# Output product of a state-space mixer: 128 rows of stacked real and imaginary parts, or 64 rows of each part

## Chip, cores and metric

One NeuronCore of a Trainium2 chip runs the whole program in one launch. The metric is the device time of that launch in microseconds (us). Engines: PE (TensorE, matmuls; PEld is its weight load), DVE (VectorE), ACT (ScalarE), POOL (GpSimd) and SP, whose queue issues all the DMAs named here.

## What is computed

One layer of a hybrid decoder on a prompt of 2048 tokens and 8 single-token samples, width 1024. The input projection feeds a state-space mixer (512 channels), a pooling mixer (512 channels) and a gate for each; an output projection, a residual and a LayerNorm follow. The change lies in the state-space mixer, which is complex and diagonal: 32 groups of 16 channels with 64 states each.

```python
bu_re = jnp.einsum('blgc,gnc->blgn', ug, bbar_re)
bu_im = jnp.einsum('blgc,gnc->blgn', ug, bbar_im)
_, _, hr, hi = lax.associative_scan(_scan_combine, (a_re, a_im, bu_re, bu_im), axis=1)
...
y = (jnp.einsum('blgn,gcn->blgc', hr, c_re.astype(f32))
     - jnp.einsum('blgn,gcn->blgc', hi, c_im.astype(f32)))
y = y.reshape(bsz, L, SSM_WIDTH) + d.astype(f32) * u
```

Here `hr`, `hi` are the states' real and imaginary parts, and both contribute to the output `y`.

## The kernel before

**Stages.** Rows of x are transposed on PE into `xh`/`xl` (each number is held as a high and a low part, and a product takes three matmuls: high by high, high by low, low by high, the list `HL`). The projection `proj` (L207) then runs tile by tile for the whole first two thirds of the program. Beside it run side tasks: `params` builds the mixer's weights, `ssm_task` the state-space mixer, `pool_diff` and `pool_gate` the pooling mixer. After 470 us come the GLU (L1058) and the output projection with LayerNorm (L1098).

**Order.** The schedule of PE, ACT, DVE and POOL is the order in which the code emits instructions. `Line` counts the matmul time emitted so far and lets each side task go on when its next due time (the numbers it yields) has come. Each engine then executes its own list strictly in that order; only SP's queue is ordered by the framework.

**The mixer.** The 2048 tokens are 256 blocks of 8 tokens. `ssm_task` goes through 16 pairs of groups (`gp`). For each pair: `ssm_load` fetches block inputs `ut` and weights by DMA; `ssm_uh` splits `ut` into high and low (`uh`, ACT L155 then DVE L149); `ssm_s` multiplies them by `ws` (PE, L629) into the block sums `s`; four ACT copies (L684) bring `s` into `SP` in the scan's layout: partition 64c+n is state n of group c of the pair, and dim 1 holds the real and imaginary part. POOL copies the sample columns to `bus` (L690). DVE rotates (`SP`, `B`), scans over the blocks in four pieces (L722, start values L716 and L718), and rotates back: two products over all 128 partitions, and then the four half-size sums that make the states `hf`:

```python
o = [hf[64 * a:64 * a + 64, c, 9:265] for c in range(2) for a in range(2)]
tt(o[0], A[p0, 0], B[p0, 1], ALU.subtract, G)
tt(o[1], A[p0, 1], B[p0, 0], ALU.add)
tt(o[2], A[p1, 0], B[p1, 1], ALU.subtract)
tt(o[3], A[p1, 1], B[p1, 0], ALU.add)
```

These move the layout: partition 64a+n of `hf` holds part a (real, imaginary) of state n, and dim 1 the group. The first runs on POOL (`G`), the other three on DVE. `hf` is split into `hh` (ACT, then DVE), and `ssm_out` (L642) multiplies `hh` by the output weights `wq` into the PSUM pair `py`, where L704 has already put the part that comes from the block's own inputs. For each group that is one product over 128 partitions, real and imaginary part stacked, so 6 matmuls of 264 columns per pair. The next pair's `uh` and `s` are emitted between scan and `hh`, and `ssm_out` of a pair comes in the scan of the next. `wq` comes from the DRAM tensor `qw_d` (4 DMAs per pair, L711), written in `params` (8 DMAs, L451). `hsh` holds the samples' start states in the layout of `hf` (L674, L735).

Of the kernel before, what the change touches and what calls it, by code (L numbers as in the profile page):

```python
# [9 lines left out]
F32 = mybir.dt.float32  # L10
# [3 lines left out]
ALU = mybir.AluOpType  # L14
# [3 lines left out]
P = 128  # L18
# [27 lines left out]
class Line:  # L46
    """Emission order: side tasks advance as the matmuls of the main stream go by."""
# [38 lines left out]
class Lock:  # L86
    """One holder at a time among the side tasks."""
# [14 lines left out]
def hybrid_step(  # L102
# [39 lines left out]
    qw_d = dram.tile([2, NST, 2, GP, 2, P], F32, name="qw_d")  # L142
# [15 lines left out]
    def cmul(out, a, z, m1, m2, sh, eng=None):  # L158
        """out = a * z, complex; a and out hold (re, im) in dim 1, z is a pair of broadcast views."""
        tt(m1, a, z[0].to_broadcast(sh), ALU.mult, eng)  # L160
        tt(m2, a, z[1].to_broadcast(sh), ALU.mult, eng)
        tt(out[:, 0], m1[:, 0], m2[:, 1], ALU.subtract, eng)
        tt(out[:, 1], m1[:, 1], m2[:, 0], ALU.add, eng)
# [57 lines left out]
    def params(tmp, prod):  # L221
# [183 lines left out]
        for g0 in range(0, GP, N2):  # L405
# [28 lines left out]
            for g in range(2):  # L434
# [16 lines left out]
            dma(out=qw_d[:, :, :, g2].rearrange("p n a g h c -> (p n) a (g h c)"),  # L451
                in_=QH.rearrange("p a g h c -> p a (g h c)").bitcast(F32))
# [186 lines left out]
    def ssm_out(gp, py, hh, wq):  # L639
        for c in range(2):  # L640
            for i, (a, b) in enumerate(HL):
                nc.tensor.matmul(out=py[:, c, 0:264], lhsT=wq[:, c, a], rhs=hh[:, b, c], start=False, stop=(i == 2))  # L642
        line.t += 0.66
        yt = sc_["sc"].tile([P, 2, 264], F32, tag="yt", name=f"yt{gp}")
        S.activation(out=yt, in_=py[:, :, 0:264], func=AF.Gelu_apprx_tanh)
        for c in range(2):
            g = 2 * gp + c
            dma(out=y_d[:, CH * g:CH * g + CH, :], in_=yt[:, c, 8:264])
        dma(out=ys_d[2 * gp:2 * gp + 2].rearrange("g c b -> c g b"), in_=yt[0:CH, :, 0:8])

    def ssm_task():
# [6 lines left out]
        bus, hs0, hsh = (sc.tile([P, 2, NB, GP], F32, name=nm) for nm in ("bus", "hs0", "hsh"))  # L658
        ssm_load(0)
        srt = sc.tile([P, 4, P], F32, tag="hh", name="srt")  # L660
        srh = srt[:, 2:4].rearrange("p a (i n) -> p a i n", i=2)
        for i, st in enumerate((state_re, state_im)):
            dma(out=srt[:, i], in_=st[0].rearrange("b (a c) n -> (b a) (c n)", c=2))
            dma(out=srh[:, :, i], in_=st[0].rearrange("b (a c) n -> (b a) c n", c=2))
# [6 lines left out]
        for i in range(4):  # L671
            transpose(ph[:, P * i:P * i + P], srt[:, i], P)
        S.copy(out=hs0.rearrange("p a b g -> p (a b g)"), in_=ph[:, 0:256])
        S.copy(out=hsh.rearrange("p a b g -> p (a b g)"), in_=ph[:, 256:512])  # L674
# [3 lines left out]
        p0, p1 = slice(0, 64), slice(64, 128)  # L678
        for gp in range(GP):
# [17 lines left out]
            for h in range(NCK // HC):  # L697
                if h == 0 and prev:
                    ssm_out(*prev)
                if h == 2:  # L700
# [8 lines left out]
                    for c in range(2):  # L709
                        for a in range(2):  # L710
                            dma(out=wq[64 * a:64 * a + 64, c].bitcast(F32), in_=qw_d[c, :, a, gp])  # L711
# [18 lines left out]
            o = [hf[64 * a:64 * a + 64, c, 9:265] for c in range(2) for a in range(2)]  # L730
            tt(o[0], A[p0, 0], B[p0, 1], ALU.subtract, G)
            tt(o[1], A[p0, 1], B[p0, 0], ALU.add)
            tt(o[2], A[p1, 0], B[p1, 1], ALU.subtract)
            tt(o[3], A[p1, 1], B[p1, 0], ALU.add)
            S.copy(out=hf[:, :, 0:8], in_=hsh[:, :, :, gp])  # L735
# [25 lines left out]
        for a, o, f in ((0, o_re_s, o_re_p), (1, o_im_s, o_im_p)):  # L761
            dma(out=o[0].rearrange("b (a c) n -> (b a) (c n)", c=2), in_=hout[:, a])
            dma(out=f[0, 0].rearrange("(a c) n -> a c n", c=2),
                in_=fout[:, :, NST * a:NST * a + NST])
# [133 lines left out]
    def pool_seq(gi, seq, hook):  # L898
        """seq: (0, i) reads chunk i of the pooled part, (1, i) of its gate."""
# [329 lines left out]
```

## Time and profile before

| what | us |
|---|---|
| median of 3 runs (lowest, highest) | 725.35 (725.2, 725.85) |
| span of the profiled execution | 721.6 |
| lies around the span, if it ran like one of the three | 3.6 to 4.25 |
| PE busy in the span | 679.6 (94%) |
| DVE busy | 513.0 (71%) |
| ACT busy | 230.9 (32%) |
| POOL busy | 210.0 (29%) |

The span reaches from the first to the last instruction; the time of that execution as a whole is not listed by itself. A busy share is an average over stages with different limits, so the stage of the mixer has to be read by itself. "L642" is a line of the kernel before.

### The profile page before, as it was taken

The numbers are of one execution on the slowest core, as the hardware profiler recorded it, in microseconds if no ns is written. First come the engines' busy times: TensorE is split into PE (matmuls) and PEld (weight loads), VectorE is DVE, ScalarE is ACT, GpSimd is POOL, SyncE is SP. The second block draws the span as 40 slices with busy tenths as digits, with TensorE's granted clock in tenths as the row PEclk, the third lists the DMA queues.
The fourth block names the chain that finished last, engine by engine and source line by source line (L and its number), as shares of the span: only waits on it lengthen the run. The fifth ranks groups of instructions, "written<-read, shape, count | busy, mean of one in ns | idle before, by whom it ended". The sixth has DMA issues, their size and how long they took to land.

```text
span 721.6 us, 10736 instructions
## 1 busy us (share of the span) xinstructions
PE 679.6 (94%) x3641; PEld 576.5 (80%) x3641; DVE 513.0 (71%) x1145; ACT 230.9 (32%) x472; POOL 210.0 (29%) x266
## 2 busy tenths in 40 slices
PE   6999999999999999979988989989999999999995
PEld 5987887888898879867876778776888868888884
DVE  3699888652789899988988895487555557646444
ACT  4442233233433333333333232354221323313100
POOL 2006435300010222222134223655313234051322
PEclk9999999999999999999998999999999999999998
DMA  8992778665555343433343224944455562634432
GB/s 286 215 355 79 173 205 206 175 226 163 165 158 163 107 141 115 139 101 102 119 131 107 86 75 122 366 146 104 111 118 137 128 174 60 148 90 115 118 87 60
DMA packets 134902, 105.99 MB, mean 147 GB/s; under 512 B 71459, under 2 KB 112551, under 8 KB 134839
## 3 DMA queue, kind: packets, MB, share of 16 engines
q1 hardware_dynamic: 134847, 105.30, 51.6%
q8 instruction: 29, 0.48, 0.3%
q14 instruction: 26, 0.21, 0.1%
HBM read 63.82 MB, written 41.68 MB: 146 GB/s over the span
## 4 chain that ended last, share of the span: by engine, by line
PE 45%; DVE 24%; ACT 5%; DMA 3%; issue 3%; POOL 2%; SPq 2%; DVEq 0%; ACTq 0%; POOLq 0%
PE o L1098 24%; PE pj L207 14%; PE z L1058 5%; DVE SP L149 4%; DVE hf L149 3%; DVE B L722 3%; POOL ws L149 2%; DVE B L149 2%; ACT SP L684 2%; DVE ini L718 2%; DVE uh L149 1%; DMA wst<-in_w_in_dram 1%; DVE w L149 1%; DVE dh L149 1%; PE os L1098 1%
## 5 line engine op out<-in xcount | busy, mean ns | idle before, releaser
L207 PE MATMUL pj<-xh,w 128*128 128x512 f32 (+2 forms) x1312 | 334.2, 348 | 0.0
L207 PEld LDWEIGHTS pj<-xh,w 128*128 128x128 f32 x1312 | 225.2, 190 | 28.7
L207 PE MATMUL pj<-xl,w 128*128 128x512 f32 (+2 forms) x656 | 206.4, 346 | 0.0
L1098 PE MATMUL o<-wo,mix 128*128 128x512 f32 (+1 forms) x792 | 176.9, 384 | 1.5 <-ACT mix L155 1.5
L1098 PEld LDWEIGHTS o<-wo,mix 128*128 128x128 f32 x792 | 145.1, 188 | 32.5 <-ACT mix L155 2.3
L207 PEld LDWEIGHTS pj<-xl,w 128*128 128x128 f32 x656 | 120.0, 189 | 14.1
L149 POOL TENSOR_TENSOR xr<-xr,gb 128x1024 f32<-128x1024 f32 x15 | 36.0, 2401 | 48.1 <-DVE xr L149 42.7
L149 POOL TENSOR_TENSOR hf<-SP,B 64x256 f32<-64x256 f32 x16 | 15.4, 960 | 108.6 <-DVE B L149 108.6
L1058 PE MATMUL z<-yh,w_g 128*128 128x512 f32 (+2 forms) x240 | 45.4, 348 | 0.0
L1087 ACT ACTIVATE xr<-xr,mv 128x1024 f32<-128x1024 f32 x15 | 18.7, 1245 | 79.4 <-DVE mv L1077 74.6
L1058 PEld LDWEIGHTS z<-yh,w_g 128*128 128x128 f32 x240 | 38.7, 188 | 6.3 <-issue 0.2
L1066 DVE SCALAR_TENSOR_TENSOR xr<-xr,o 128x512 f32<-128x512 f32 (+1 forms) x33 | 22.0, 667 | 26.1 <-PE o L1098 26.1
L149 POOL TENSOR_TENSOR ws<-ws 128x525 f32<-128x525 f32 (+5 forms) x30 | 37.8, 1259 | 3.3 <-DVE dh L149 1.1
L149 POOL TENSOR_TENSOR ws<-pc 128x527 f32<-128x527 f32 (+1 forms) x20 | 20.4, 1018 | 56.8 <-ACT pc L813 20.3
L155 ACT CAST hh<-hf 128x528 fp32r<-128x528 f32 x16 | 10.1, 634 | 76.5 <-DVE hf L149 72.6
L149 DVE TENSOR_TENSOR xl<-pt,xh 128x1024 fp32r<-128x1024 f32 (+1 forms) x17 | 19.8, 1164 | 16.5 <-ACT xh L155 16.2
L149 POOL TENSOR_TENSOR mv<-mv,mhalf 128x1 f32<-128x1 f32 x16 | 9.9, 619 | 74.2 <-DVE mv L1072 74.2
L722 DVE TENSOR_TENSOR_SCAN B<-r,ini,SP 128x64 f32<-128x64 f32 x96 | 29.9, 353 | 0.0
L149 DVE TENSOR_TENSOR hf<-SP,B 64x256 f32<-64x256 f32 x48 | 28.4, 591 | 1.0
L149 DVE TENSOR_TENSOR yh<-y,yh 128x512 fp32r<-128x512 f32 (+2 forms) x20 | 12.2, 610 | 21.6 <-ACT yh L155 19.1
L149 DVE TENSOR_TENSOR mix<-y,mix 128x512 fp32r<-128x512 f32 (+2 forms) x20 | 18.3, 915 | 12.1 <-ACT mix L155 12.1
L690 POOL COPY bus<-SP 128x16 f32<-128x16 f32 x16 | 8.8, 550 | 60.3 <-ACT SP L684 60.3
(220 smaller groups left out, 915.9 us busy)
## 6 DMA issues: line engine op xcount, KB each, us to landing
wst<-in_w_in_dram SPq DMA_DIRECT2D x16, 512.0 KB
xr<-in_x_prompt_dram SPq DMA_DIRECT2D x24, 256.0 KB
out_dram<-xr SPq DMA_DIRECT2D x22, 256.0 KB
xw<-in_x_prompt_dram SPq DMA_DIRECT2D x8, 512.0 KB
wt_d<-wzero SPq DMA_DIRECT2D x4, 1024.0 KB
sw_d<-sv SPq DMA_DIRECT2D x8, 512.0 KB
qw_d<-qh SPq DMA_DIRECT2D x8, 512.0 KB
ws<-sw_d SPq DMA_DIRECT2D x16, 256.0 KB
```

The costliest lines, as they stand in the source:

```text
L149: (eng or V).tensor_tensor(out=out, in0=a, in1=b, op=op)
L155: S.copy(out=hi, in_=src)
L207: nc.tensor.matmul(out=ps[:, :n], lhsT=w[:, a, k], rhs=xcols(b, k, t0, n), start=(i == 0), stop=(i == 23))
L684: S.copy(out=SP[64 * c:64 * c + 64, a], in_=ps[64 * a:64 * a + 64, c, 0:264])
L690: G.tensor_copy(out=bus[:, :, :, gp], in_=SP[:, :, 256:264])
L718: V.scalar_tensor_tensor(out=it[:, a], in0=e[:, 1 - a], scalar=z7[:, 2 - a, gp:gp + 1], in1=it[:, a], op0=ALU.mult, op1=ALU.add)
L722: V.tensor_tensor_scan(out=B4[:, a, h], data0=dec, data1=A4[:, a, h], initial=ini[a], op0=ALU.mult, op1=ALU.add)
L1058: nc.tensor.matmul(out=ps[:, :n], lhsT=w[:, a, k, P * (m % 2):P * (m % 2) + P], rhs=yh[:, b, k, :n], start=(i == 0), stop=(i == 11))
L1066: V.scalar_tensor_tensor(out=xt[:n, c], in0=xt[:n, c], scalar=ALPHA, in1=ps, op0=ALU.mult, op1=ALU.add)
L1087: S.activation(out=xt[:n], in_=xt[:n], func=AF.Identity, scale=mv[:n, 2:3], bias=mv[:n, 0:1])
L1098: nc.tensor.matmul(out=ps, lhsT=lhs(a, k), rhs=wo_view(k)[:, b, 512 * h + c.start:512 * h + c.stop], start=(i == 0), stop=(i == len(hl) * ...
```

## The change

The states keep the layout of the scan: partition 64c+n, part in dim 1. The back rotation ends in two DVE operations over 128 partitions, and none on POOL. The product for group c then takes rows 64c to 64c+63 of `hh` and `wq`, real and imaginary part one after the other into the same PSUM columns: 12 matmuls of 264 columns with 64 rows each, the two groups in turn. `qw_d` and `wq` are laid out to suit (16 DMAs to write, one per pair to read), and `hsh` with its copy, its loads and two transposes goes.

```diff
-    qw_d = dram.tile([2, NST, 2, GP, 2, P], F32, name="qw_d")
+    qw_d = dram.tile([GP, P, 2, 2, P], F32, name="qw_d")
...
-            dma(out=qw_d[:, :, :, g2].rearrange("p n a g h c -> (p n) a (g h c)"),
-                in_=QH.rearrange("p a g h c -> p a (g h c)").bitcast(F32))
+            for g in range(N2):
+                dma(out=qw_d[g0 + g], in_=QH[:, :, g].bitcast(F32))
...
     def ssm_out(gp, py, hh, wq):
-        for c in range(2):
-            for i, (a, b) in enumerate(HL):
-                nc.tensor.matmul(out=py[:, c, 0:264], lhsT=wq[:, c, a], rhs=hh[:, b, c], start=False, stop=(i == 2))
+        for i in range(6):
+            r, (a, b) = i % 2, HL[i // 2]
+            for c in range(2):
+                cs = slice(64 * c, 64 * c + 64)
+                nc.tensor.matmul(out=py[:, c, 0:264], lhsT=wq[cs, r, a], rhs=hh[cs, b, r], start=False, stop=(i == 5))
...
-        bus, hs0, hsh = (sc.tile([P, 2, NB, GP], F32, name=nm) for nm in ("bus", "hs0", "hsh"))
+        bus, hs0 = (sc.tile([P, 2, NB, GP], F32, name=nm) for nm in ("bus", "hs0"))
...
-        for i in range(4):
+        for i in range(2):
             transpose(ph[:, P * i:P * i + P], srt[:, i], P)
         S.copy(out=hs0.rearrange("p a b g -> p (a b g)"), in_=ph[:, 0:256])
-        S.copy(out=hsh.rearrange("p a b g -> p (a b g)"), in_=ph[:, 256:512])
...
-                    for c in range(2):
-                        for a in range(2):
-                            dma(out=wq[64 * a:64 * a + 64, c].bitcast(F32), in_=qw_d[c, :, a, gp])
+                    dma(out=wq.bitcast(F32), in_=qw_d[gp])
...
-            o = [hf[64 * a:64 * a + 64, c, 9:265] for c in range(2) for a in range(2)]
-            tt(o[0], A[p0, 0], B[p0, 1], ALU.subtract, G)
-            tt(o[1], A[p0, 1], B[p0, 0], ALU.add)
-            tt(o[2], A[p1, 0], B[p1, 1], ALU.subtract)
-            tt(o[3], A[p1, 1], B[p1, 0], ALU.add)
-            S.copy(out=hf[:, :, 0:8], in_=hsh[:, :, :, gp])
+            tt(hf[:, 0, 9:265], A[:, 0], B[:, 1], ALU.subtract)
+            tt(hf[:, 1, 9:265], A[:, 1], B[:, 0], ALU.add)
+            S.copy(out=hf[:, :, 0:8], in_=hs0[:, :, :, gp])
...
-            dma(out=f[0, 0].rearrange("(a c) n -> a c n", c=2),
-                in_=fout[:, :, NST * a:NST * a + NST])
+            dma(out=f[0, 0].rearrange("(a c) n -> a (c n)", c=2), in_=fout[:, a])
```

On DVE, before, the end of the scan of one pair and the split of its states (`SP`, `B`: rotated sums; `hh`: high and low part of `hf`):

```order
L149 TENSOR_TENSOR uh_4504<-ut,uh_4504 128x544
L149 TENSOR_TENSOR SP_4389<-B_4394,tbl_4287 128x2x256
L149 TENSOR_TENSOR B_4394<-B_4394,tbl_4287 128x512
L149 TENSOR_TENSOR hf<-SP_4389,B_4394 64x256 x3
L149 TENSOR_TENSOR hh_4529<-hf,hh_4529 128x528
```

The same place with the change:

```order
L149 TENSOR_TENSOR uh_4516<-ut,uh_4516 128x544
L149 TENSOR_TENSOR SP_4398<-B_4403,tbl_4301 128x2x256
L149 TENSOR_TENSOR B_4403<-B_4403,tbl_4301 128x512
L149 TENSOR_TENSOR hf<-SP_4398,B_4403 128x256 x2
L149 TENSOR_TENSOR hh_4539<-hf,hh_4539 128x528
```

Two operations over 128 partitions stand where three over 64 stood, and on POOL the fourth is gone; nothing changes place on PE, ACT, DVE or POOL.

On PE, before, the same pair's output product between two tiles of the projection (`pj`):

```order
L207 MATMUL pj_1536_4561<-xl_88,w_3607 128x256
L207 MATMUL pj_1536_4561<-xh_86,w_3607 128x256 x2
L642 MATMUL y_4447<-hh_4529,wq_4465 128x264 x6
L207 MATMUL pj_1536_4561<-xh_86,w_3607 128x256 x6
L207 MATMUL pj_1024_4618<-xh_86,w_4157 128x512
```

With the change:

```order
L207 MATMUL pj_1536_4571<-xl_88,w_3614 128x256
L207 MATMUL pj_1536_4571<-xh_86,w_3614 128x256 x2
L644 MATMUL y_4462<-hh_4539,wq_4480 128x264 x12
L207 MATMUL pj_1536_4571<-xh_86,w_3614 128x256 x6
L207 MATMUL pj_1024_4634<-xh_86,w_4167 128x512
```

The product has 12 matmuls in the place of 6.

## Rows read from the trace of the kernel before

**Rows 1.** Two stretches: busy us (instructions) of PE, PEld, DVE, ACT, POOL; PE clock, DMA.

```profile
176.00:249.97 73.97, 73.97 (x429) 65.26 (x427) 59.08 (x160) 28.80 (x67) 8.92 (x28) 1.00 0.50 151
249.97:438.59 188.62, 171.08 (x949) 146.16 (x948) 171.47 (x399) 63.27 (x154) 51.03 (x66) 0.98 0.37 111
```

**Rows 2.** The longest wait of PE from 250 to 438.6 us: total us, times, longest.

```profile
PE s L629 <- DVE uh L149: 7.8, 6, 2.8
```

**Rows 3.** Stretches from one product s (L629) to the next, columns as in group 1.

```profile
249.97:265.99 16.02, 14.73 (x71) 11.74 (x69) 15.65 (x35) 5.10 (x12) 3.86 (x5) 1.00 0.44 137
265.99:281.04 15.05, 14.72 (x85) 12.77 (x84) 13.68 (x35) 4.79 (x12) 2.47 (x4) 1.00 0.37 110
281.04:297.63 16.59, 15.20 (x112) 14.17 (x110) 15.14 (x41) 6.80 (x18) 2.79 (x4) 1.00 0.39 119
297.63:311.52 13.89, 13.89 (x70) 11.77 (x69) 11.81 (x30) 5.10 (x11) 4.67 (x6) 1.00 0.46 136
311.52:329.97 18.45, 14.75 (x70) 11.74 (x69) 17.12 (x35) 6.05 (x15) 7.04 (x7) 1.00 0.40 118
329.97:346.03 16.06, 15.02 (x88) 12.94 (x87) 14.07 (x37) 5.45 (x13) 3.20 (x5) 1.00 0.32 98
346.03:362.35 16.32, 15.60 (x108) 14.12 (x107) 15.95 (x41) 6.20 (x15) 3.48 (x5) 1.00 0.39 116
362.35:379.21 16.86, 14.55 (x70) 11.57 (x68) 14.51 (x36) 6.15 (x15) 6.04 (x8) 1.00 0.41 121
379.21:398.52 19.31, 16.46 (x69) 13.65 (x70) 17.09 (x28) 5.07 (x13) 8.50 (x9) 0.82 0.38 113
398.52:415.44 16.92, 15.12 (x92) 13.13 (x90) 14.85 (x39) 5.38 (x13) 3.96 (x6) 1.00 0.26 80
415.44:438.59 23.15, 21.04 (x129) 18.56 (x128) 21.59 (x55) 7.17 (x19) 5.01 (x8) 1.00 0.28 84
```

**Rows 4.** Timeline of DVE, then POOL, at one pair's states: start, us, engine, line.

```profile
401.86 1.74 DVE L149 TENSOR_TENSOR hf<-SP,B 64x256 f32<-64x256 f32 x3
...
401.90 0.97 POOL L149 TENSOR_TENSOR hf<-SP,B 64x256 f32<-64x256 f32 x1 [3.83 <-DVE B L149]
```

**Rows 5.** Tiles hf and sp: duration ns min/median/max, first and last start.

```profile
L149 DVE TENSOR_TENSOR hf<-SP,B x48: 420/423/1889, 190.7 to 435.4; 64x256 f32<-64x256 f32 x48
L149 DVE TENSOR_TENSOR sp<-sp,sp x16: 417/425/461, 72.6 to 154.1; 128x256 f32<-128x256 f32 x16
```

**Rows 6.** Timeline of PE at one output product.

```profile
388.77 0.89 PE L642 MATMUL y<-hh,wq 128*128 128x264 f32 x6
389.50 0.39 PE L207 MATMUL pj<-xl,w 128*128 128x512 f32 x1
```

**Rows 7.** Timeline of PE at eight narrow transposes (8 rows), and their group (mean ns).

```profile
54.79 0.63 PE L207 MATMUL pj<-xh,w 128*128 128x512 f32 x2
55.35 0.66 PE L146 MATMUL pt<-ident,xst 8*128 8x8 f32 x8
55.93 1.45 PE L207 MATMUL pj<-xh,w 128*128 128x512 f32 x5
...
L146 PE MATMUL pt<-ident,xst 8*128 8x8 f32 x8 | 0.7, 204 | 0.0
```

**Rows 8.** Timeline of PE at eight full transposes (128 rows).

```profile
42.51 1.03 PE L146 MATMUL pt<-ident,xst 128*128 128x128 f32 x8
43.30 0.48 PE L207 MATMUL pj<-xh,w 128*128 128x512 f32 x1
```

**Rows 9.** DMA issues of lines 711 and 451 on SP: ns min/median/max.

```profile
L711 SPq DMA_DIRECT2D wq<-qw_d x64: 444/588/1562, 180.3 to 426.9; - x64
L451 SPq DMA_DIRECT2D qw_d<-qh x8: 518/519/1796, 80.8 to 158.8; - x8
```

**Rows 10.** Timeline of DVE, then POOL, where both work on sums.

```profile
369.62 2.37 DVE L149 TENSOR_TENSOR SP<-SP,B 128x256 f32<-128x256 f32 x2
...
370.59 2.32 POOL L149 TENSOR_TENSOR ws<-ws 128x525 f32<-128x525 f32 x2
```

More of the change, by code (lines that the diff above doesn't have):

```diff
@@ L657, in ssm_task @@
         sc, ut, hf = sc_["sc"], sc_["ut"], sc_["hf"]
-        bus, hs0, hsh = (sc.tile([P, 2, NB, GP], F32, name=nm) for nm in ("bus", "hs0", "hsh"))
+        bus, hs0 = (sc.tile([P, 2, NB, GP], F32, name=nm) for nm in ("bus", "hs0"))
         ssm_load(0)
-        srt = sc.tile([P, 4, P], F32, tag="hh", name="srt")
-        srh = srt[:, 2:4].rearrange("p a (i n) -> p a i n", i=2)
+        srt = sc.tile([P, 2, P], F32, tag="hh", name="srt")
         for i, st in enumerate((state_re, state_im)):
             dma(out=srt[:, i], in_=st[0].rearrange("b (a c) n -> (b a) (c n)", c=2))
-            dma(out=srh[:, :, i], in_=st[0].rearrange("b (a c) n -> (b a) c n", c=2))
         yield 12.0
@@ L677, in ssm_task @@
         sh = [P, 2, NCK // HC, HC]
-        p0, p1 = slice(0, 64), slice(64, 128)
         for gp in range(GP):
```

## The prediction

> **What bounds the kernel now.** The page's busy shares come first: PE is busy for nearly the whole span, so a gain can come only from where PE waits, and work that is added to PE is paid in full wherever it does not wait. The stretches come second, because the mixer's stage is two stages. From 176 to 250 us PE is busy for all 73.97 us and DVE for 59.08: PE sets the pace. From 250 to 438.6 us, when the pooling sums have joined, PE is busy for 171.08 of 188.62 us and DVE for 171.47 [rows 1]. PE idles 17.5 us there, and the waits say for whom: the longest is that of the product s for the DVE half of `uh`, 7.8 us in 6 waits [rows 2]. DVE's list is full, the next pair's `uh` stands behind everything in it, and PE stops when it arrives at s too early. So the second stretch is DVE's, the first PE's. The third view cuts the second stretch at each s: PE's idle time is the length less its busy time, from 0 (the fourth) to 3.70 us (the fifth), and sums to 17.5 over eleven stretches [rows 3].
>
> **What DVE and POOL save.** The three half-size sums of `hf` last 1.74 us as a row of three, and the POOL sum beside them 0.97 us [rows 4]. One of them undisturbed takes 0.42 us [rows 5]; so two make 0.85, and the third stands 0.89 us, just about as long as POOL works at the same time. I read this as DVE held while POOL reads its two operands. The new sums cover 128 partitions with the same 256 columns. Operations of that very shape, `sp` in the weight stage, take 0.425 us in the median [rows 5], as much as the half-size ones. Two without POOL then take 0.85 us: 0.89 us less per pair, and the POOL sum goes. In sixteen pairs that is 14.2 us of DVE. It shortens the way that matters: the ACT half of `hh`, and behind it on ACT the copies of the next s into `SP`, wait for `hf`, and the next rotation on DVE waits for those.
>
> **What PE pays.** Today the six matmuls take 0.73 us, 0.122 each, from 388.77 to 389.50 [rows 6]. Of the twelve, each has half the rows and the same 264 columns. If the two groups' matmuls do not overlap, the block takes 12 x 0.122 = 1.46 us; if they do, six times 0.122, unless the twelve weight loads are slower. The trace has no pair of matmuls on different rows. It does have eight narrow transposes on 8 rows, each with its own load of a full 128 columns: they start (0.66 - 0.20)/7 = 0.066 us apart [rows 7], so twelve loads need at most 0.79 us. I take 0.79, nearest to what twelve short instructions on part of the rows do here. Going into and out of the narrow form costs something as well. Before the narrow transposes a projection matmul starts at 55.03 (54.79 plus 0.63 less its 0.39), the usual step is 0.24, and they start at 55.35: 0.08 lost. The last one starts at 55.81 and the projection at 55.93, 0.05 more than a step; its five matmuls take 1.45 where 4 x 0.24 + 0.39 = 1.35: 0.10 more [rows 6, 7]. Together 0.23. So the block takes 1.02 instead of 0.73: c = 0.29 us more per pair.
>
> On the weight loads the Trainium skill speaks against the change: "TensorE: Matmul & The Clock Gate", section "LDWEIGHTS (loading the stationary operand)", gives columns divided by 1.2 ns whatever the number of rows, so about 107 ns for 128 columns. The narrow transposes do not agree, with 0.066 us for load and matmul together [rows 7], and the measurement decides. By the page twelve loads would take 1.28 us instead of 0.79 and the sum would come to about 724.5.
>
> **The sum.** Where PE has idle time, a pair gains the smaller of 0.89 and (idle less c); where it has none, it loses c. For the eleven stretches, idle 1.29, 0.33, 1.39, 0, 3.70, 1.04, 0.72, 2.31, 2.85, 1.80, 2.11 [rows 3], with c = 0.29, that is 0.89 seven times, 0.04, -0.29, 0.75 and 0.43: 7.16 us. The other five products (four before 250 us, where PE never idles [rows 1], and the last one at 438.59) cost 5 x 0.29 = 1.45. Two transposes fewer at the start give back 2 x 0.10 [rows 8]. Net 5.9 us. The span of 721.6 would become 715.7, and since the runs' median of 725.35 lies 3.75 above that span, I forecast **719.5**.
>
> **Edits that I cost at nothing.** SP issues 64 loads of `wq`, 0.588 us each [rows 9]; sixteen larger ones remain, which frees some 1.8 us per pair of a queue whose transfers are needed a pair later. The writes of `qw_d` become sixteen, eight more at about 0.52 us [rows 9], over some 80 us; SP is ahead of the mixer there, and PE shows no idle time after 176 us [rows 1] that a late weight could have made. If that cover went, it would be 4 us once. The copy of `hsh` is one small ACT instruction. With the POOL sum gone, ACT and DVE get waits of their own on POOL, for the preceding pair's copy to `bus`, which was issued a whole pair earlier; queued behind them are the copies into `SP` and the rotation.
>
> **Rivals.**
>
> *The twelve run one after another (slower).* Place: the output product. Price: 12 x 0.122 + 0.23 - 0.73 = 0.96 us per pair. The same sum gives 0.33, -0.63, 0.43, -0.96, 0.89, 0.08, -0.24, 0.89, 0.89, 0.84, 0.89, or 3.41, less 5 x 0.96, plus 0.2: 1.2 us slower, 726.5, and 724 to 729 as stretches pass time on to one another. It decides from a block of about 1.6 us on, 0.113 per matmul. For it: no row shows two matmuls overlapping on different rows. Against it: the matmuls alternate between the upper and the lower 64 rows and write to different banks. It is also the case that the change does not do what its order is made for. At the far end, each alternation costs the 0.08 of a change of form: 12 x 0.2 us, c = 1.9, and 739.
>
> The page "TensorE: Matmul & The Clock Gate", section "Part 3: Packing small matmuls", says that matmuls on different row groups run at the same time, a few ns apart; no run so far shows it. By it six pairs take about 0.76 us.
>
> *The loads take the pace of full transposes.* Those start (43.30 - 42.51)/8 = 0.10 us apart [rows 8], each with a 128-column load. Then c = 12 x 0.10 + 0.23 - 0.73 = 0.70 and the gain falls to 1.7 us: 723.6. Against it: the narrow ones [rows 7]. This is the mechanism of the page's rule on loads above.
>
> *The collision moves instead of going.* POOL's pooling sums hold DVE too: two sums that need 0.85 last 2.37 us beside them [rows 10]. If POOL, freed of its wait, now meets some other DVE work, DVE saves one operation, 0.42 per pair, and the sum is 0.42 in nine stretches, 0.04, -0.29, less 1.45, plus 0.2: 2.3 us, 723.1. Against it: the pooling sums are no more and no longer than before.
>
> *Saved time is carried over.* If DVE keeps its lead across stretches, all eleven gain 0.89: 9.8 - 1.45 + 0.2 = 8.5 us, 716.8. In the ninth stretch the granted clock is 0.82 [rows 3], 36% of 19.31 us at 1.2 instead of 2.4 GHz, after PE had idled; if the shorter wait keeps the clock up, up to 3.5 us more: 713.3.
>
> **How the numbers follow.** Forecast 0.47; one after another 0.14, with its far end 0.03; slower loads 0.11; moved collision 0.11; carried over 0.14. A measurement of this kernel tells 0.2%, 1.45 us, from no change, so faster means below 723.9 and slower above 726.8. Faster: nearly all of the forecast, all of carried over, some two thirds of the two weak gains: 0.73. Slower: half of one after another, its far end, and a little of the loads: 0.11. The same: 0.16. The range from 715.0 to 727.0 leaves out the lower half of carried over, the upper half of one after another and its far end: under 0.2.
>
> **What would show it.** The two new `hf` sums at 0.85 us per pair, and DVE's busy time about 14 us lower in all; the output product, from its first start to the next projection matmul, at 0.8 to 1.0 us (0.79 plus what of the form change lies inside; 1.5 or more is the slower rival); PE's idle time from 250 us to the last product down from 17.5 to about 7 us, with s waiting for `uh` far below 7.8. Wrong would be the forecast if the block stayed near 1.5 us, if other DVE rows grew by as much as `hf` shrank, or if PE idled as long as before, for something other than `uh` and `hh`.

## The result, and the profile after

The changed kernel takes **714.95 us** in the median of four runs (712.72 to 716.31) against 725.59 of four runs of the kernel before beside it: a ratio of 0.9862, 95% interval 0.9844 to 0.9879. A second comparison gave 713.19 against 725.84, 0.9831 (0.9805 to 0.9857). It is faster by 10.6 and 12.7 us where 5.9 were forecast; 714.95 lies a hair below the range's low end of 715.0, and 713.19 lies 1.8 below it. The profiled execution took 712.72 us with a span of 710.9; the span before was 721.6, so the spans differ by 10.7 us. In every run that lists both, the time is 1.7 to 1.9 us longer than the span. The profile before is therefore of an execution of about 723.4 us, 2 us under the median of 725.35, and not 3.6 to 4.25 us longer than its span; the forecast's step of 3.75 from span to median was in part this difference between executions.

Where they went is read from the same two stretches as before, cut at the first product s, the sixth, and the last output product (length, then busy us and instructions of PE, PEld, DVE, ACT, POOL; PE clock; DMA):

```profile
176.74:252.25 75.51, 75.51 (x452) 65.16 (x451) 57.90 (x159) 28.79 (x66) 6.46 (x25) 1.00 0.50 149
252.25:428.07 175.82, 171.06 (x1015) 146.54 (x1013) 157.77 (x385) 65.06 (x154) 39.17 (x53) 0.98 0.40 118
```

Against [rows 1] the first stretch is 1.3 us longer (75.51 for 74.20; its front end lies at the first s, at 175.77, where [rows 1] cut at 176). PE still fills it. The second is 12.8 shorter (175.82 for 188.62), and DVE's busy time in it 13.7 lower (157.77 for 171.47). PE's busy time is the same to 0.02, so its idle time went from 17.5 to 4.8. What lies before the first s grew by 1.0 and what lies behind the last product shrank by 0.1: -10.7 in all. The 1.0 is not shown to be the change's: over all the profiles of this study that start lies anywhere from 175.8 to 178.7.

The waits of PE in the second stretch, with [rows 2] as their counterpart:

```profile
PE s L629 <- DVE uh L149: 3.6, 2, 2.8
PE s L629 <- ACT uh L155: 0.9, 1, 0.9
PE y L644 <- DVE hh L149: 0.2, 1, 0.2
```

Of 7.8 us in six waits 3.6 in two are left. The stretches from one s to the next, which answer one by one to [rows 3]:

```profile
252.25:266.63 14.38, 14.38 (x77) 11.75 (x75) 13.68 (x34) 5.61 (x13) 2.29 (x3) 1.00 0.54 162
266.63:281.46 14.83, 14.83 (x91) 12.83 (x90) 12.53 (x33) 5.93 (x16) 1.49 (x3) 1.00 0.37 113
281.46:296.62 15.16, 15.16 (x117) 14.25 (x116) 13.81 (x39) 6.08 (x16) 1.72 (x3) 1.00 0.43 121
296.62:310.90 14.28, 14.28 (x76) 11.75 (x75) 12.11 (x32) 6.13 (x13) 4.67 (x6) 1.00 0.43 122
310.90:325.89 14.99, 14.70 (x77) 11.79 (x75) 13.71 (x30) 5.09 (x12) 5.94 (x6) 1.00 0.50 146
325.89:341.77 15.88, 15.12 (x94) 12.97 (x93) 13.94 (x36) 5.89 (x14) 1.66 (x4) 1.00 0.34 104
341.77:356.83 15.06, 15.06 (x114) 14.05 (x113) 14.44 (x40) 6.21 (x16) 2.51 (x4) 1.00 0.41 123
356.83:372.13 15.30, 14.45 (x77) 11.56 (x75) 13.15 (x33) 5.97 (x13) 5.08 (x7) 1.00 0.44 132
372.13:392.53 20.40, 17.55 (x76) 14.17 (x76) 18.43 (x35) 5.15 (x13) 7.93 (x8) 0.83 0.37 109
392.53:407.46 14.93, 14.93 (x98) 13.18 (x96) 12.99 (x33) 5.99 (x14) 3.16 (x7) 1.00 0.38 109
407.46:428.07 20.61, 20.61 (x135) 18.25 (x133) 19.00 (x50) 7.01 (x18) 2.72 (x5) 1.00 0.23 78
```

PE now has no idle time in seven of the eleven (length equals busy) where it had none in one. Length before less length after, and the forecast's term for it:

| stretch | 1 | 2 | 3 | 4 | 5 | 6 | 7 | 8 | 9 | 10 | 11 | sum |
|---|---|---|---|---|---|---|---|---|---|---|---|---|
| gained, us | 1.64 | 0.22 | 1.43 | -0.39 | 3.46 | 0.18 | 1.26 | 1.56 | -1.09 | 1.99 | 2.54 | 12.80 |
| forecast | 0.89 | 0.04 | 0.89 | -0.29 | 0.89 | 0.75 | 0.43 | 0.89 | 0.89 | 0.89 | 0.89 | 7.16 |

Seven gained more than the 0.89 that was taken for a ceiling. The one large stall left is in the ninth stretch, which had it before too and lost 1.09 (experiments e8 and e9). Neighbouring stretches trade such amounts: in a second profile of the changed kernel the ninth takes 19.08 us and the tenth 16.01.

The states of one pair, to be read beside [rows 4] (timeline; start, us), and all sums of that kind (count, then ns min/median/max), beside [rows 5]:

```profile
408.15 0.76 DVE L149 TENSOR_TENSOR hf<-SP,B 128x256 f32<-128x256 f32 x2
...
409.01 0.63 ACT L155 CAST hh<-hf 128x528 fp32r<-128x528 f32 x1 [2.35 <-DVE hf L149]
```

```profile
L149 DVE TENSOR_TENSOR hf<-SP,B x32: 414/424/1171, 191.5 to 423.8; 128x256 f32<-128x256 f32 x32
```

Two sums in 0.76 us (they overlap by 0.09) stand where three took 1.74. DVE's groups of these sums in the second stretch, first of the kernel before, then of the changed one (count, then busy us, mean ns, idle before):

```profile
L149 DVE TENSOR_TENSOR hf<-SP,B 64x256 f32<-64x256 f32 x36 | 21.5, 598 | 0.7
```

```profile
L149 DVE TENSOR_TENSOR hf<-SP,B 128x256 f32<-128x256 f32 x24 | 10.6, 485 | 0.4
```

That is 10.9 us of the 13.7. The other 2.8 are for the most part work that was done earlier: in the first stretch these sums fell by 3.3 us (6.8 to 3.5) and DVE's busy time by only 1.2 (59.08 to 57.90), because DVE already makes the products of five back rotations there, where it made those of four before. The last product in the first stretch, first of the kernel before, then of the changed one:

```profile
L149 DVE TENSOR_TENSOR B<-B,tbl 128x512 f32<-128x512 f32 x4 | 2.8, 692 | 0.1
```

```profile
L149 DVE TENSOR_TENSOR B<-B,tbl 128x512 f32<-128x512 f32 x5 | 4.2, 841 | 0.2
```

Over both stretches DVE's busy time fell by 14.9 us (230.5 to 215.7), of which the sums are 14.2. POOL works 11.9 us less in the second (39.17 for 51.03).

The output product, beside [rows 6]:

```profile
411.52 1.00 PE L644 MATMUL y<-hh,wq 64*128 64x264 f32 x12
412.45 0.38 PE L207 MATMUL pj<-xh,w 128*128 128x256 f32 x1
```

The twelve occupy 0.93 us from their first start to the next projection matmul, instead of 0.73. The single starts in the trace come in pairs 3 to 4 ns apart (411.742 and 411.745, 411.866 and 411.869), one pair every 0.122 us, which is the step of one matmul on 128 rows before.

### The profile page after: what moved, and what is told of

It is laid out like the page before. It is cut to its first block, busy times and chain, and to the rows that moved or that the text cites. A ratio compares the mean times of both kernels' runs of the same rounds, so it can differ in the third digit from the quotient of the medians.

```text
span 710.9 us, 10871 instructions
## 1 busy us (share of the span) xinstructions
PE 682.5 (96%) x3735; PEld 578.5 (81%) x3735; DVE 497.5 (70%) x1129; ACT 232.7 (33%) x471; POOL 195.5 (27%) x250
## 4 chain that ended last, share of the span: by engine, by line
PE 63%; DVE 12%; ACT 3%; POOL 2%; DMA 2%; issue 2%; SPq 1%; DVEq 0%; ACTq 0%; POOLq 0%
PE pj L207 28%; PE o L1090 24%; PE z L1050 5%; POOL ws L149 2%; DVE SP L149 2%; DVE B L718 1%; PE y L644 1%; PE s L629 1%; PE os L1090 1%; PE y L702 1%; ACT SP L682 1%; PE pm L854 1%; DVE B L149 1%; DVE ini L714 1%; DVE w L149 1%
## 5 line engine op out<-in xcount | busy, mean ns | idle before, releaser
L207 PEld LDWEIGHTS pj<-xl,w 128*128 128x128 f32 x656 | 120.3, 190 | 14.9
L1050 PE MATMUL z<-yh,w_g 128*128 128x512 f32 (+2 forms) x240 | 47.0, 356 | 0.0
L149 POOL TENSOR_TENSOR ws<-pc 128x527 f32<-128x527 f32 (+1 forms) x20 | 21.9, 1096 | 91.0 <-ACT pc L805 39.6
L149 DVE TENSOR_TENSOR xl<-pt,xh 128x1024 fp32r<-128x1024 f32 (+1 forms) x17 | 19.8, 1164 | 17.4 <-ACT xh L155 17.3
L149 DVE TENSOR_TENSOR yh<-y,yh 128x512 fp32r<-128x512 f32 (+2 forms) x20 | 12.2, 610 | 21.7 <-ACT yh L155 21.7
L149 DVE TENSOR_TENSOR xr<-xr,gb 128x1024 f32<-128x1024 f32 x15 | 18.3, 1220 | 10.5 <-ACT xr L1079 10.5
L682 ACT COPY SP<-s 64x264 f32<-64x264 f32 x64 | 23.8, 372 | 3.8 <-PE s L629 3.2
```

Of the source, the lines that this page charges most:

```text
L149: (eng or V).tensor_tensor(out=out, in0=a, in1=b, op=op)
L207: nc.tensor.matmul(out=ps[:, :n], lhsT=w[:, a, k], rhs=xcols(b, k, t0, n), start=(i == 0), stop=(i == 23))
L682: S.copy(out=SP[64 * c:64 * c + 64, a], in_=ps[64 * a:64 * a + 64, c, 0:264])
L1050: nc.tensor.matmul(out=ps[:, :n], lhsT=w[:, a, k, P * (m % 2):P * (m % 2) + P], rhs=yh[:, b, k, :n], start=(i == 0), stop=(i == 11))
```

## The experiments

The first theory after the result, **carried over**: in the second stretch every pair goes once round a chain that runs mainly through DVE (copies of s into `SP`, rotation, scan, `hf`, `hh`, the next `uh`), and what is taken off that chain adds up from pair to pair. Its rival, **capped**: a pair can gain at most 0.89 and at most what PE idles in its own stretch, and the other half of the gain has another source (the product itself, SP's queue, POOL). The first four kernels split the change into its parts. Beside them the kernel before had a median of 724.85 us.

**e1: the new product alone**, on the kernel before; on the old layout it multiplies other halves of weights and states than the reference does.

```diff
-        for c in range(2):
-            for i, (a, b) in enumerate(HL):
-                nc.tensor.matmul(out=py[:, c, 0:264], lhsT=wq[:, c, a], rhs=hh[:, b, c], start=False, stop=(i == 2))
+        for i in range(6):
+            r, (a, b) = i % 2, HL[i // 2]
+            for c in range(2):
+                cs = slice(64 * c, 64 * c + 64)
+                nc.tensor.matmul(out=py[:, c, 0:264], lhsT=wq[cs, r, a], rhs=hh[cs, b, r], start=False, stop=(i == 5))
```

> The kernel before with the new product alone: 12 matmuls of 64 rows in the place of 6, on the old layout of the states, so it leaves half of the products out and takes the others in their place (the output is not the mixer's). Theory (DVE sets the pace from 250 us, PE before): the block costs 0.39 us more per pair as in the changed kernel; 5 pairs pay it in full (2.0 us), the 11 in the mixed stretch for the most part inside waits: 726.5 to 729, that is 1 to 3.5 us slower than before. Rival (the product itself is part of the gain): 720 to 724, faster than before.

Measured: 724.47 us, ratio 0.9998 (0.9986 to 1.0010). A miss, no loss at all. The first stretch grew as the price says, from 74.20 to 75.73: four products at 0.38, by the starts of s, 14.63 apart instead of 14.25. The second did not:

```profile
252.07:438.91 186.84, 175.39 (x1015) 149.05 (x1013) 169.83 (x396) 63.57 (x154) 50.99 (x66) 0.96 0.37 112
```

It is 1.8 us shorter, though PE is busy 4.3 us longer. So PE's price is paid only where PE sets the pace, and the new product is not where the gain comes from. DVE is 1.6 us less busy there because it had done the work before: in the longer first stretch it is busy for 60.59 us instead of 59.08, with the products of five back rotations instead of four. Over both stretches it is busy for 230.4 us, as before (230.5), and their length is 262.6 for 262.8. A lead that DVE wins while PE sets the pace is kept across the cut.

**e2: the saving on the sums alone**, on the kernel before: two of the four sums of `hf` are left out (`hf` is set to zero at the start).

```diff
-            tt(o[0], A[p0, 0], B[p0, 1], ALU.subtract, G)
             tt(o[1], A[p0, 1], B[p0, 0], ALU.add)
             tt(o[2], A[p1, 0], B[p1, 1], ALU.subtract)
-            tt(o[3], A[p1, 1], B[p1, 0], ALU.add)
```

> The kernel before with two of its four half-size sums left out (the POOL one and one of DVE's), so half of the states stay zero. Theory: the row of sums falls from 1.74 to 0.85 us per pair as in the changed kernel, with nothing added on PE; the mixed stretch (188.6 us) shrinks by what DVE's busy time shrinks, 11 to 13 us, so 711 to 714.5, at or below the changed kernel. Rival (the gain comes from the loads of wq and the queue of SP): 724 to 726, no change.

Measured: 714.03 us, 0.9844 (0.9830 to 0.9859). A hit: leaving out one sum on DVE and the one on POOL gives the whole gain.

```profile
251.10:427.50 176.40, 167.02 (x950) 145.58 (x949) 160.01 (x385) 64.03 (x154) 38.34 (x53) 0.98 0.39 118
```

The first stretch stayed at 74.20, the second fell by 12.2 us with DVE's busy time down by 11.5.

**e3: POOL's sum moved to DVE**, on the kernel before.

```diff
-            tt(o[0], A[p0, 0], B[p0, 1], ALU.subtract, G)
+            tt(o[0], A[p0, 0], B[p0, 1], ALU.subtract)
```

> The kernel before with the POOL sum on DVE: four half-size sums in a row on DVE, none on POOL. Theory (POOL's sum holds DVE for as long as one sum takes): the row lasts 4 x 0.42 = 1.69 us instead of 1.74, and the time stays within 1.5 us of before, 724 to 727. Rival (POOL's sum is free beside DVE, and the first DVE sum is long for another reason): the row lasts 0.89 + 3 x 0.42 = 2.15 us, 0.42 more per pair, and the time rises by 4 to 6 us, 729.5 to 731.5.

Measured: 724.41 us, 0.9997 (0.9982 to 1.0012). A hit: a fourth sum on DVE costs what POOL's help had cost it.

```profile
L149 DVE TENSOR_TENSOR hf<-SP,B x64: 418/421/1165, 192.0 to 436.1; 64x256 f32<-64x256 f32 x64
```

All four now take 0.42 us each, 1.68 a pair, beside the 1.74 of [rows 4].

**e4: one load of `wq` per pair**, on the kernel before (`qw_d` in an order that allows it, written by 32 DMAs).

```diff
-                    for c in range(2):
-                        for a in range(2):
-                            dma(out=wq[64 * a:64 * a + 64, c].bitcast(F32), in_=qw_d[c, :, a, gp])
+                    dma(out=wq.bitcast(F32), in_=qw_d[gp].rearrange("a n c h o -> (a n) c h o"))
```

> The kernel before with wq loaded by one DMA per pair instead of four, from a DRAM tensor written by 32 DMAs instead of 8; nothing else changes. Theory: SP's queue is not on the path, 724.5 to 727. Rival (the shorter queue of SP is where the gain comes from): 715 to 721.

Measured: 726.28 us, 1.0019 (1.0007 to 1.0031). A hit: SP's queue gave nothing, if anything it lost 1.4 us.

The next four take the changed kernel apart. The kernel before had 725.84 us beside them, the changed kernel itself 713.19.

**The changed kernel again**, for a second profile.

> The changed kernel once more, for a second profile on the chip of the next three. Both theories of the gain (what VectorE saves is carried from pair to pair through the whole second stretch; or it is capped by TensorE's idle time pair by pair) must take its time as it comes: 713 to 716 us, against 725 for the kernel before. What a second profile can tell: if the second stretch is VectorE's busy time plus 17 to 18 us in it too (175.82 against 157.77 in the first profile), the carried-over theory stands; a stretch that differs by over 2 us at equal busy time speaks for chance in how the queues meet.

Measured: 713.19 us, 0.9831 (0.9805 to 0.9857); second stretch 176.54 us with DVE busy for 158.55, 18.0 more. As expected.

**e5: the six matmuls of one half of the rows in a row.**

```diff
-        for i in range(6):
-            r, (a, b) = i % 2, HL[i // 2]
-            for c in range(2):
-                cs = slice(64 * c, 64 * c + 64)
+        for c in range(2):
+            cs = slice(64 * c, 64 * c + 64)
+            for i in range(6):
+                r, (a, b) = i % 2, HL[i // 2]
```

> The changed kernel with its twelve 64-row matmuls in another order: the six of one half of the rows, then the six of the other. If two neighbours share the array only because they stand on different rows, the block takes 12 steps of about 0.122 instead of 6: 1.65 us from its first matmul to the next projection's instead of 0.925, +0.73 a pair. Then the first stretch (five products, TensorE without idle time) grows by 3.6 us to 79, and in the second TensorE's work (171.06 + 11 x 0.73 = 179) passes the 175.8 that the stretch has: 179 to 184 there; 715 + 3.6 + 3 to 8 = 722 to 727 us. If order does not matter (loads hidden, each matmul at half the columns' cost), the block stays at 0.92 and the time at 713 to 716.

Measured: 715.95 us, 0.9857 (0.9828 to 0.9886). Neither: the block took half of the way to the serial one.

```profile
199.65 1.36 PE L644 MATMUL y<-hh,wq 64*128 64x264 f32 x12
200.94 0.50 PE L207 MATMUL pj<-xl,w 128*128 128x512 f32 x1
```

1.29 us against 0.93, 0.36 more, three steps of 0.12. The starts tell why. Two series run side by side: 199.651, .878, .999, 200.120, .241, .358 and 200.005, .231, .355, .477, .600, .728, each with the steps 0.227 and about 0.12 that a series has alone. The second half's matmuls started when the first half had done three of its six: neighbours on other rows do run at once, and the alternation is needed only for the three that were not reached in time. (Which series a start belongs to is inferred from its step; the trace does not name the rows.) In the first stretch the 0.35 per product were paid in full (76.89 for 75.51); the second as a whole grew by 0.2 to 1.0 (176.77, with PE 2.5 us busier than in the first profile of the changed kernel). Its median lies 2.8 us above the changed kernel's, more than the stretches show, but the intervals overlap.

**e6: eight of the twelve.**

```diff
-        for i in range(6):
+        for i in range(4):
...
-                nc.tensor.matmul(out=py[:, c, 0:264], lhsT=wq[cs, r, a], rhs=hh[cs, b, r], start=False, stop=(i == 5))
+                nc.tensor.matmul(out=py[:, c, 0:264], lhsT=wq[cs, r, a], rhs=hh[cs, b, r], start=False, stop=(i == 3))
```

> The changed kernel with eight of the twelve 64-row matmuls; it leaves out the low half of the weights times the high half of the states. Each pair has two steps of 0.122 less on TensorE. First stretch: -5 x 0.244 = -1.2 us by both theories. Second stretch, 11 products: if VectorE's busy time still sets it, 0 to -0.5, and the time is 713.5 (715 - 1.2 - 0.3); if TensorE sets it now, -2.7, and the time is 711.

Measured: 712.42 us, 0.9814 (0.9795 to 0.9834); the first stretch 74.54, 0.98 less (it holds four products, not the five I counted); the second 175.33, 0.5 to 1.2 less than in the two profiles of the changed kernel, where DVE's reading had 0 to 0.5 and PE's 2.7. The time lies between the two expectations, 713.5 and 711. The stretches one by one, behind e11, show why: in five of them PE does set the pace.

**e8: a weight split behind the next `uh`**, against the ninth stretch's stall.

```diff
-                line.add(w_in_task(9 + gi))
+                line.add(w_in_task(9 + gi, 8.2 if gi == 2 else 6.4))
```

> The changed kernel, with the split of one weight block (tile w_11) emitted behind the splits of the next pair's input and states instead of ahead of them. In the profile of the changed kernel this split (2.04 us, while GpSimd works on ws) holds the input split that the thirteenth product s waits for, and TensorE stands for about 4 us there and runs at half clock for 2 more. If that stall is lost time, the run takes 709 to 712 us (715 less 3 to 6). If VectorE's busy time sets the second stretch as a whole, its work is only reordered, the stall moves to another pair, and the time stays at 714 to 716.

Measured: 712.97 us, 0.9825 (0.9801 to 0.9848), as the changed kernel beside it (713.19); the expected 714 to 716 started from 715. The stall stayed: the eighth stretch became 1.0 us shorter (14.33) and the ninth stayed long (20.91). First DVE at that place (timeline) in the changed kernel, then in e8, then what PE waited for in e8's second stretch:

```profile
371.77 2.04 DVE L149 TENSOR_TENSOR w<-wst,w 128x1024 fp32r<-128x1024 f32 x1
373.73 1.58 DVE L149 TENSOR_TENSOR uh<-ut,uh 128x544 fp32r<-128x544 f32 x1
```

```profile
371.97 1.07 DVE L712 TENSOR_SCALAR ini<-B,z 128x2 f32<-128x2 f32 x1
373.07 1.22 DVE L714 SCALAR_TENSOR_TENSOR ini<-B,z,ini 128x1 f32<-128x1 f32 x2
374.22 1.45 DVE L718 TENSOR_TENSOR_SCAN B<-r,ini,SP 128x64 f32<-128x64 f32 x2
375.60 0.69 DVE L149 TENSOR_TENSOR uh<-ut,uh 128x544 fp32r<-128x544 f32 x1
```

```profile
PE s L629 <- DVE uh L149: 4.3, 2, 3.5
```

POOL's pooling sums run there from 371.95 to 375.28 in e8. With the weight split gone from there, the start values and the scan, which stand ahead of `uh` in both kernels, ran beside those sums and were drawn out instead: the same three rows take 0.23, 0.35 and 0.59 us in the changed kernel, from 370.75 to 371.86, where POOL's sums start at 371.67.

The last four ask what POOL's work costs DVE, and whether the second stretch follows DVE when something else on it changes. The kernel before had 724.93 us beside them.

**e7: one of the two new sums on POOL.**

```diff
-            tt(hf[:, 0, 9:265], A[:, 0], B[:, 1], ALU.subtract)
+            tt(hf[:, 0, 9:265], A[:, 0], B[:, 1], ALU.subtract, G)
```

> The changed kernel with the first of its two hf sums on GpSimd. If GpSimd's sum holds VectorE (in the kernel before, the first of three sums took about as long as GpSimd's 0.97 beside it), the one hf sum left on VectorE takes 0.9 to 1.0 us where both took 0.76 to 0.85 together, VectorE saves nothing, and the time is 713 to 717 us. If the engines work freely side by side, the sum left takes 0.42, VectorE's busy time falls by 16 x 0.42 = 6.7, and the time by 3 to 5, to 709 to 711.

Measured: 716.17 us, 0.9882 (0.9864 to 0.9900): the time of the hold theory, but not for its reason.

```profile
L149 DVE TENSOR_TENSOR hf<-SP,B x16: 425/426/1172, 190.6 to 424.4; 128x256 f32<-128x256 f32 x16
L149 POOL TENSOR_TENSOR hf<-SP,B x16: 912/977/987, 190.7 to 424.4; 128x256 f32<-128x256 f32 x16
```

DVE's sum takes 0.43 us beside POOL's, which in fourteen pairs starts 0.04 to 0.12 after it: it is not held. What ACT waits for in the second stretch (us in total, times, longest):

```profile
ACT hh L155 <- POOL hf L149: 42.6, 11, 6.6
```

The split `hh` now waits for POOL's sum, which ends about 1.0 us after the first sum's start, where the two on DVE ended after 0.76; so the split starts 1.06 us after the sums do, for 0.85. (The total of the wait says nothing here: in the changed kernel the same split waits 43.3 us in all for DVE.)

```profile
251.38:428.93 177.55, 171.15 (x1015) 146.12 (x1014) 154.39 (x372) 64.66 (x154) 51.52 (x65) 0.98 0.39 117
```

DVE is 3.4 to 4.2 us less busy than in the two profiles of the changed kernel and the stretch 1.0 to 1.7 longer. So it is not the sum of DVE's work that sets the stretch, but the chain in which DVE stands: taking work off DVE gained nothing where the next step then had to wait longer for POOL.

**e9 and e10: the pooling's running sums (`ws`) on DVE**, in the changed kernel and in the kernel before.

```diff
-            tt(nx[:, lo:16 + n], cur[:, lo:16 + n], cur[:, lo - d:16 + n - d], ALU.add, G)
+            tt(nx[:, lo:16 + n], cur[:, lo:16 + n], cur[:, lo - d:16 + n - d], ALU.add)
```

> The changed kernel with the pooling's running sums (tiles ws) on VectorE instead of GpSimd. In its second stretch these are 28 operations and 31.4 us of GpSimd; on VectorE, at 0.69 for 512 columns and 0.37 for 256, some 15.4 us more. In the profile of the changed kernel VectorE's operations there take 23 us more in all than at their undisturbed length. If that is GpSimd's hold, VectorE's busy time falls by about 8, to 150; then TensorE is the bound, the stretch is 171 to 174 us instead of 176, and the time 710 to 713. If GpSimd's work is a real help to VectorE, its busy time rises by up to 15, and the time goes to 722 to 730.

> The kernel before with the same edit: the pooling's running sums on VectorE, nothing else. No part of the state output changes, so this asks whether VectorE's busy time alone sets the second stretch. There its operations take 30 us over their undisturbed length, some 7 of it beside GpSimd's hf sums, which stay. By the hold theory its busy time falls from 171.5 by about 8; if the stretch is that plus 17, it falls from 188.6 to 181, and the time to 717 to 719 us. If the saving is capped by TensorE's idle time pair by pair, it is 3 to 5 at most: 720 to 722. If GpSimd helps: over 730.

Measured: e9 713.04 us, 0.9839 (0.9822 to 0.9856), as the changed kernel; e10 722.24 us, 0.9956 (0.9940 to 0.9972). The second stretch of e9, then of e10:

```profile
253.55:428.30 174.75, 169.98 (x1015) 145.67 (x1013) 156.69 (x414) 64.94 (x154) 9.11 (x25) 0.99 0.40 119
```

```profile
250.53:436.60 186.07, 171.05 (x949) 146.97 (x948) 168.46 (x427) 63.48 (x154) 19.56 (x37) 0.98 0.38 112
```

Both times lie above what the hold theory gave (710 to 713 and 717 to 719), because its size was wrong: with 28 or 29 operations more on it, DVE's busy time fell by 1.1 and 3.0 us, not by 8. POOL's busy time fell by 30 and 31 us, and that work had saved DVE nothing. e10 leaves the state output as it was, and its second stretch falls by 2.6 us with DVE's 3.0; but 722.24 lies next to the 720 to 722 of the capped reading, so e10 by itself does not decide between the two.

**e11: e9 with eight of the twelve** (the diffs of e9 and e6 together).

> The kernel with the pooling's running sums on VectorE and, as in the run with eight matmuls, without the low half of the weights times the high half of the states. There the four matmuls less, 0.24 us a pair on TensorE, took the second stretch down by 0.5 to 1.2 us of the 2.7 that 11 pairs carry. If TensorE is the bound once VectorE is relieved, they are now worth 2.2 to 2.7 there and 1.0 in the first stretch: 3.2 to 3.7 us below the run that has only the sums moved. If VectorE still sets it, 1 to 2 us below.

Measured: 710.23 us, 0.9803 (0.9784 to 0.9821), 2.8 below e9, between the two expectations. The profile decides: the first stretch is 74.54, 0.97 less, and the second

```profile
250.81:424.83 174.02, 168.13 (x971) 143.66 (x969) 156.61 (x414) 64.56 (x154) 8.83 (x25) 0.98 0.40 120
```

0.7 less than in e9, of the 2.7 that 11 products carry. The rest of the 2.8 lies outside the two stretches and in the scatter of the runs.

The single stretches tell who sets which. Lengths in us from one s to the next; a star marks those in which PE is shown without idle time:

| stretch | 1 | 2 | 3 | 4 | 5 | 6 | 7 | 8 | 9 | 10 | 11 |
|---|---|---|---|---|---|---|---|---|---|---|---|
| after | 14.38* | 14.83* | 15.16* | 14.28* | 14.99 | 15.88 | 15.06* | 15.30 | 20.40 | 14.93* | 20.61* |
| after, again | 14.37* | 14.84* | 15.15* | 14.28* | 15.25 | 15.91 | 15.06* | 15.28 | 19.08 | 16.01 | 21.31 |
| e2 | 13.97* | 14.44* | 14.76* | 13.89* | 16.21 | 15.51 | 15.07* | 15.95 | 18.89 | 16.06 | 21.65 |
| e5 | 14.73* | 15.20* | 15.54* | 14.62* | 14.89 | 15.87 | 15.42* | 14.62* | 19.07 | 15.85 | 20.96* |
| e6 | 14.12* | 14.59* | 14.91* | 14.03* | 15.18 | 15.89 | 14.82* | 15.70 | 18.87 | 15.79 | 21.43 |
| e9 | 14.38* | 14.83* | 15.16* | 14.28* | 14.49* | 14.89* | 15.49 | 15.03 | 19.51 | 14.91* | 21.78 |

Stretches 1 to 4 of the changed kernel are PE's: they are the same to 0.01 in both profiles and with DVE's load changed (e9), 0.24 to 0.26 shorter with two steps of 0.122 fewer (e6), and 0.34 to 0.38 longer with the slower block (e5). The seventh follows PE in e5 and e6 in the same way. In the others PE mostly waits for DVE's chain, they differ from profile to profile, and what PE gains or loses in the five is partly lost or made up there. So the second stretch, which was DVE's in all but the fourth, is shared by both engines after the change.

The whole second stretch in the kernels that change DVE's or PE's work, in us:

| kernel | before | e1 | e2 | e3 | after | e5 | e6 | e8 | e9 | e10 | e11 | e7 |
|---|---|---|---|---|---|---|---|---|---|---|---|---|
| length | 188.6 | 186.8 | 176.4 | 188.1 | 175.8 | 176.8 | 175.3 | 175.6 | 174.8 | 186.1 | 174.0 | 177.6 |
| DVE busy | 171.5 | 169.8 | 160.0 | 171.0 | 157.8 | 157.2 | 158.2 | 157.8 | 156.7 | 168.5 | 156.6 | 154.4 |
| difference | 17.2 | 17.0 | 16.4 | 17.1 | 18.1 | 19.6 | 17.1 | 17.9 | 18.1 | 17.6 | 17.4 | 23.2 |

It is DVE's busy time and 16 to 20 us in which DVE waits, but for e7, where the chain leaves DVE for POOL. In the changed kernel some of these waits are for PE's pace, so the sum describes the stretch and does not say that DVE alone sets it. No kernel that computes everything beat the changed one: e8 and e9 equal it.

## Why the prediction was right in direction and short in size

**What bounds the kernel: held for the kernel before.** First stretch PE's, second DVE's. e1 shows it from PE's side (a price on PE counts in the first stretch and not in the second), e2 and e10 from DVE's. It no longer holds after the change: PE then sets the first four stretches and the seventh of the second part (e5, e6), and relieving DVE in e9 leaves those four as they are.

**The sums: held.** 0.89 a pair forecast; 10.9 us over the twelve pairs of the second stretch measured, 0.91 each, with the new sums at 0.424 us where 0.425 was taken. DVE's busy time fell by 15.5 us over the span (14.2 forecast), 14.7 of it in the sums. That DVE was held while POOL read held in effect (e3), but is finer than I put it; see the last section.

**The product: right in kind, mis-sized.** The block was to be 0.8 to 1.0 and is 0.93. The term of twelve loads, 0.79, is 6 x 0.122 = 0.73, set by the matmuls and not by the loads (eight take 0.69, twelve 0.93: 0.06 each). The term of the change of form, 0.23 from transposes on 8 rows, is about 0.38: into the form 0.09 more than a step, the first pair 0.10 more, out of it 0.09, and the first projection matmul 0.10. So c is 0.38, not 0.29. With 0.38 and 0.22 the prediction's own sum would have come to 5.1 us instead of 5.9: the price that was too small hid a part of the error in the sum below. The two transposes gave back 0.22 (0.2 forecast): the first s-to-s distance is 16.64 for 16.86. Together 4 x 0.38 - 0.22 = 1.3, the first stretch's 1.3.

On the loads the Trainium skill's rule, "TensorE: Matmul & The Clock Gate", section "LDWEIGHTS (loading the stationary operand)", would have made the block 1.28 us if its twelve loads follow one another, which is an estimate; the trace has 0.93 and does not agree. Its section "Part 3: Packing small matmuls" has matmuls on other rows start some 4 ns apart; the trace agrees, with 3 to 4 ns.

**The sum: this step failed.** "A pair gains the smaller of 0.89 and (idle less c)" gives 7.16 us; the stretch gave 12.8. Two readings were wrong in it.

First, the ceiling of 0.89 by stretch: DVE's list is one line, and a lead won in one pair is kept for the next. Of the 13.7 us that DVE's busy time lost, 12.8 came off the stretch, where the cap would have let 7.2 pass; the fourth stretch had no idle time to give, and the fifth gained 3.46. e2, which has no price on PE, decides it: there the cap lets 8.2 us pass (0.89 or the idle time, whichever is less), and the stretch gave 12.2. That is the rival *saved time is carried over*, to which I gave 0.14 at 716.8: it is what happened.

Second, the idle time of [rows 3] is less than what PE lost. With the sums alone (e2) stretches 1 to 3 fell to 13.97, 14.44 and 14.76 us, by 2.05, 0.61 and 1.83, where PE was shown idle for 1.29, 0.33 and 1.39: a matmul's shown end reaches into the wait behind it. With the product in place the same stretches are 0.39 to 0.41 longer, and that is c, paid in full. The Trainium skill says of this that the shown end of a matmul is an estimate from its size ("Perfetto Trace Analysis", section "Tensor Engine Instruction (MATMUL, LD_WEIGHTS)"); the trace agrees, with these gains beyond the idle time.

Even carried over, the forecast would have been 8.5 us of the span's 10.7. That rival counted the leads of the eleven stretches alone. The sums of the four pairs in the first stretch were not in it: DVE is not the bound there, but it used the time to work ahead across the cut, and about 2.1 of the 2.8 us beyond the sums stand in the first stretch instead. How the remaining 2 us divide between this lead and the rest of DVE's rows is not shown.

**Costed at nothing: held.** SP's loads and writes (e4). The added waits on POOL's copy show in no wait of PE or DVE.

**Rivals.** One after another: fell (0.93 us). Loads at the transposes' pace: fell. The collision moves: fell as a whole, though e8 shows a collision moving from one row to its neighbour. The clock part of carried over did not come in the first profile: the ninth stretch has a granted clock of 0.83 for 0.82, since its stall stayed. In the second profile it has 0.91, but the tenth stretch then waits, and the whole is no shorter (176.54).

**Left open.** Which single waits make up the whole of DVE's 17 us before: 12.4 are waits for ACT, 5.7 of them for its half of `hh`; the rest is gaps that no listed wait explains. Why stretches 5 to 11 differ by up to 1.3 us between two profiles of one kernel is open too.

## What to carry to other kernels

Find out first which engine's list a stage follows, and then sum what the change takes off that chain over the whole stage, not pair by pair: leads are kept, even from the stage before, and the idle time shown on the engine that waits is too small to serve as a cap. What ends the gain is the other engine's own pace, and it should be looked up stretch by stretch: here PE sets five of eleven after the change. Work given to a helper engine counts at what the chain then waits for; here POOL's share was worth nothing, for the sums in the old layout (e3) and in the new one (e7) and for the pooling (e9, e10). A price on an engine that doesn't set a stretch is free there and paid in full where that engine does.

## What the runs showed of the hardware that was not expected

POOL's hold falls on the next operation. In the kernel before, all sixteen pairs have a first DVE sum of 0.42 us, already running when POOL's starts, then one of 0.85 to 0.87 (1.89 once), then one of 0.42. At 401.86 us [rows 4] the second runs from 402.30 to 403.16, and POOL's sum ends in between, at 402.88. In fourteen pairs of e7 the only sum is already running when POOL's starts, and takes 0.43. The Trainium skill calls the port that the two engines share an exclusive lock and no split of bandwidth ("Trainium Architecture — The Big Picture", section "What this means for kernel authors"); the trace agrees in that the second sum takes just one sum's length more, but a sum that was already running beside POOL's was not lengthened.

Matmuls on two halves of the rows are two series that need not be issued in turn: in e5, by the steps of the starts, the second began three steps early, before the fourth matmul of the first. And a visit to the 64-row form between 128-row matmuls costs some 0.38 us beside its steps, with twelve matmuls in it as with eight: with twelve matmuls s comes every 14.63 us for 14.25 with the same six steps of 0.122, and with eight every 14.40 with two steps fewer, 0.39.
